# A hybrid mLSTM and GLA block: output gate units in another place, sigmoid and silu from tanh

## The chip, the cores and the metric

The kernel runs on one core of a Trainium2 chip. Its time is the device time of one execution in microseconds (us). Before the change the median of three runs is 948.4 us (947.27 to 948.83).

## The reference

A block of width 1024 on 512 tokens with 16 learned meta tokens ahead of them, so 528 columns are computed. After an RMS norm, one large projection feeds two mixers of four heads each. The first mixer is an mLSTM, the second a gated linear attention (GLA). Learned gates merge the two, an output projection and a SwiGLU channel mixer follow. What the change touches:

```python
mqk = jax.nn.silu(causal_depthwise_conv(jnp.concatenate([mq, mk], axis=-1), conv_w[l], conv_b[l]))
...
hm = mlstm_chunkwise(...)
hm = head_rmsnorm(from_chunks(hm), m_head_g[l]) * jax.nn.sigmoid(mo.astype(f32)).reshape(bsz, tp, M_HEADS, M_DV)
...
merged = (jax.nn.sigmoid(gate_m) * (y_m @ w_branch_m[l].astype(dt))
          + jax.nn.sigmoid(gate_g) * (y_g @ w_branch_g[l].astype(dt)))
```

`mq` and `mk` are the queries and keys of the first mixer, one tile of 128 channels per head; `mv` its values and `mo` its output gates, two tiles per head. Everything is fp32.

## The kernel before

The activations stand channel by channel: x transposed lies in eight tiles of 128 partitions by 528 columns. The weights come from HBM as 192 units of 128 x 1024, one for each 128 output channels, and the time goes into multiplying these units with the activations. An fp32 product is made of three matmuls (L302 to L304). For that every operand is split into a high part, rounded to fp32r, and the low rest. Of a weight unit, ACT makes the high part (`whi`, L188) and DVE the low part (`wlo`, L193), a few units ahead of PE. Some later products are done in pairs, with fewer matmuls on combinations of two units (L344 to L346). There ACT copies (`sink_of`, L404 to L409) empty a PSUM bank before PE can go on in it. There are 8 banks.

`job_list` (L52) writes down the order of the units: `gates`, then for each head of the first mixer `mq`, `mk`, two `mv`, two `mo`; then pairs for the merge gates (`gm`), the second mixer, its merge gates (`gg`), and so on. PE works through the units in this order.

All work that is not a unit's own matmuls is written as Python generators. `unit` (L308) advances them eight times while it issues its own 48 matmuls: `tick` (L153) gives a step to each generator in `side`, and to the first one in `mixers`. So the position of an instruction in its engine's order depends on the units that stand before it. Each engine executes its own order strictly one after the other: an instruction that waits holds up all that stand behind it on this engine.

The generators that matter here. `conv` (L705): the depthwise convolution of one query or key tile; the PSUM result goes to SBUF (L593, two halves on DVE), the first step runs on ACT, three more on DVE (L716). `conv_act` (L720): silu on ACT (L725) once query and key are there, then the high part on ACT (L730) and the low part on DVE (L732). `gates_of` (L610) scales an `mo` tile on DVE (L615) and applies its function on ACT. `normed_x` puts x's norm to use; its steps are L508 and L517 on DVE and L511 and a further one on ACT. `mlstm` (L867) is one head's mixer; it begins with an ACT cast of a constant selector, `sel` (L872), and six ticks later PE multiplies by it (L875, L876). `head_out` (L785) ends a head: head norm with Ln and Exp, times the gate. `branch` (L1081) multiplies a merge gate and a branch product.

ACT can apply one function only while a set of tables that holds it is loaded. `act` (L126) loads the set with Exp and Ln (an instruction at L130) where it is needed. The compiler puts in the loads for silu and sigmoid, which show up at L132, the line of the activation itself.

Of the kernel before, what the change touches and what calls it, by code (L numbers as in the profile page):

```python
# [8 lines left out]
F32 = mybir.dt.float32  # L9
# [6 lines left out]
P = 128  # L16
# [6 lines left out]
H = 4  # L23
# [22 lines left out]
NSTD = 6  # L46
HA = NT - 256
LOGEXP = "natural_log_exp_and_others"
TABLE = {AF.Exp: LOGEXP, AF.Ln: LOGEXP, AF.Silu: "silu", AF.Sigmoid: "sigmoid"}


def job_list():  # L52

    one = lambda *a: [(x,) for x in a]
    o = one(("gates", 0))
    for h in range(H):
        o += one(("mq", h), ("mk", h), ("mv", 2 * h), ("mv", 2 * h + 1), ("mo", 2 * h), ("mo", 2 * h + 1))
    two = lambda n, i: [((n, 2 * i), (n, 2 * i + 1))]
    g = lambda h: [(("gq", h), ("gk", h))] + two("gv", h) + two("gr", h)
    bm = lambda i: one(("bm", 2 * i), ("bm", 2 * i + 1))  # L60
    o += two("gm", 0) + two("gm", 1) + g(0) + two("gm", 2) + two("gm", 3)
    for i in range(4):
        o += bm(i)
    q, v, r = ([g(h)[i] for h in range(H)] for i in range(3))
    o += [q[1], v[1], q[2], r[1], v[2], q[3], v[3], r[2], r[3]]
    for i in range(4):
        o += two("gg", i)
    for i in range(8):
        o += one(("bg", i))
    for i in range(8):  # L70
        o += one(("out", i))
    for m in range(FT):
        o += one(("fg", m), ("fu", m)) if m < NSTD else [(("fg", m), ("fu", m))]
    for i in range(22):
        o += one(("down", i))
    return o
# [24 lines left out]
def hybrid_block(ctx: ExitStack, tc: tile.TileContext, xT, wst, par, con, out):  # L101
# [23 lines left out]

    def act(o, i, func, **kw):  # L126
        want = TABLE.get(func)
        if want is not None and want != table[0]:
            if want == LOGEXP:
                S.preload_act_table_set(want)  # L130
            table[0] = want
        S.activation(o, i, func, **kw)  # L132

    class Box:
# [251 lines left out]
    def sink_of(boxes, a_all, b_all, func=None):  # L386

        def sink(bz, bx, by):
            every = a_all or b_all
            n = lambda full: NT if full else NS  # L390
            a, b = tt(n=n(a_all)), tt(n=n(b_all))
            sa, sb = tt(), tt()
            h2 = slice(NM, HA) if every else slice(0, 256)
            h1 = lambda full: slice(0, HA) if full else h2
            m = lambda full: HA if full else 256

            def fin():
                if func is not None:
                    act(a, a, func)
                    act(b, b, func)  # L400
                boxes[0].v, boxes[1].v = a, b

            return dict(
                s1=lambda: S.copy(sa[:, :m(a_all)], bx[:, h1(a_all)]),  # L404
                s2=lambda: S.copy(sb[:, :m(b_all)], bx[:, h1(b_all)]),
                s5=lambda: S.copy(sa[:, HA:], bx[:, h2]),
                s7=lambda: S.copy(sb[:, HA:], bz[:, h2]),
                c11=lambda: V.tensor_tensor(a[:, :m(a_all)], by[:, h1(a_all)], sa[:, :m(a_all)], ALU.add),
                c12=lambda: S.copy(a[:, m(a_all):], bx[:, h2]),  # L409
                c21=lambda: V.scalar_tensor_tensor(b[:, :m(b_all)], bz[:, h1(b_all)], -1.0, sb[:, :m(b_all)],  # L410
                                                   ALU.mult, ALU.subtract),
                c22=lambda: V.scalar_tensor_tensor(b[:, m(b_all):], sa[:, HA:], -1.0, sb[:, HA:],
                                                   ALU.mult, ALU.subtract), fin=fin)
        return sink
# [195 lines left out]
    def gates_of(boxes, pss, func):  # L610
        ts = []
        for i, scale in pss:
            t = tt(n=NS)
            if scale is not None:
                V.tensor_tensor(t, i, scale[:, NM:], ALU.mult)  # L615
                i = t
                yield 1
            ts.append((t, i))
        for b, (t, i) in zip(boxes, ts):
            act(t, i, func)  # L620
            b.v = t


# [96 lines left out]
    def conv_act(q, k, src):  # L720
        while src[0].v is None or src[1].v is None:
            yield 1
        yield 2
        for b, a in ((q, src[0].v), (k, src[1].v)):
            act(a, a, AF.Silu)  # L725
        yield 1
        for b, a in ((q, src[0].v), (k, src[1].v)):
            n = a.shape[1]
            hi, lo = tt(F32R, n), tt(F32R, n)
            S.copy(hi, a)  # L730
            yield 2
            V.tensor_tensor(lo, a, hi.bitcast(F32), ALU.subtract)  # L732
            b.v = hi, lo
        src[0].v = src[1].v = None

# [49 lines left out]
    def head_out(num, d2, gcol, gates, hd, dst):  # L785
        s0, s1 = tt(n=NS), tt(n=NS)
        act(s0, num[0], AF.Square)
        act(s1, num[1], AF.Square)
        while gates[0].v is None or gates[1].v is None:
            yield 1  # L790
        yield 1
        ts = []
        for vt in range(2):
            f = 2 * hd + vt
            t = gates[vt].v
            V.scalar_tensor_tensor(t, num[vt], pr[:, gcol + f:gcol + f + 1], t, ALU.mult, ALU.mult)
            gates[vt].v = None
            ts.append(t)
            yield 1
        V.tensor_tensor(s0, s0, s1, ALU.add)  # L800
        yield 1
        sh, sl = tt(F32R, NS), tt(F32R, NS)
        S.copy(sh, s0)
        yield 2
        V.tensor_tensor(sl, s0, sh.bitcast(F32), ALU.subtract)
        yield 6
        ss = bank()
        T.matmul(ss, onesr, sh, start=True, stop=False)
        T.matmul(ss, onesr, sl, start=False, stop=True)
        yield 2  # L810
        x, y0, t = tt(n=NS), s0, s1
        if d2 is not None:
            V.scalar_tensor_tensor(x, d2, 256.0 * EPS, ss, ALU.mult, ALU.add)
        else:
            V.tensor_scalar(x, ss, 256.0 * EPS * QS2, None, op0=ALU.add)
        yield 1
        act(y0, x, AF.Ln, scale=1.0 / 256.0)
        yield 1
        act(y0, y0, AF.Exp, scale=-0.5)
        yield 1  # L820
        act(t, y0, AF.Square)
        yield 1
        V.scalar_tensor_tensor(t, t, -0.5 / 256.0, x, ALU.mult, ALU.mult)
        V.scalar_tensor_tensor(y0, t, 1.5, y0, ALU.add, ALU.mult)
        yield 1
        for vt in range(2):
            y = ts[vt]
            if dst is yg and hd > 0:
                y = hpool[0].tile([P, NS], F32, tag="h", name=nm("h"))
            V.tensor_tensor(y, ts[vt], y0, ALU.mult)  # L830
            dst[2 * hd + vt] = y
            yield 1

# [117 lines left out]


    atts = []
    nega = cpool.tile([P, H], F32, name="nega")
    S.mul(nega, pr[:, C_A2B:C_A2B + H], -1.0)

# [123 lines left out]

    def branch(box, ps, sg, add=None, parts=None):  # L1081
        t = sg.v
        V.tensor_tensor(t, ps, t, ALU.mult)
        if add is not None:
            V.tensor_tensor(t, t, add.v, ALU.add)
            add.v = None
        box.v = t
        sg.v = None
        yield 1
        if parts is not None:  # L1090
            hi, lo = tt(F32R, NS), tt(F32R, NS)
            S.copy(hi, t)
            yield 1
            V.tensor_tensor(lo, t, hi.bitcast(F32), ALU.subtract)
            parts[0].append(hi)
            parts[1].append(lo)
            box.v = None
# [24 lines left out]
    def hold(what, i, boxes, func):  # L1122

        held[what] = held.get(what, []) + [unit_real((what, i))]
        if i % 2:
            run(gates_of(boxes, held.pop(what), func))
# [39 lines left out]
    for job in JOBS[2:]:  # L1166
# [3 lines left out]
        if len(job) == 2:  # L1170
# [7 lines left out]
            if what == "gq":  # L1178
                pair(job, X.w, ALL, sink_of((b.q, b.k), False, True))
            elif what == "gv":  # L1180
                pair(job, X.w, ALL, sink_of(b.vf, True, True))
            elif what == "gr":
                pair(job, X.w, REAL, sink_of(b.gates, False, False, AF.Silu))
            else:
                if what == "gg" and i == 6:
                    run(some_parts(yg, 2))
                elif what == "gm" and i == 4:
                    run(some_parts(ym, 4))
                pair(job, X.w, REAL, sink_of({"gm": gm, "gg": gg}[what][i:i + 2], False, False, AF.Sigmoid))
        elif what == "mq":  # L1190
            b = head("m", i)
            b.src = [box(), box()]
# [17 lines left out]
                fetch_mix()  # L1210
                fetch_mix()
        elif what == "mo":
            hold(what, i, head("m", i // 2).gates, AF.Sigmoid)
        elif what == "bm":
            while not hpool:
                tick()
# [392 lines left out]
```

## Time and profile before

| | |
|---|---|
| median of 3 runs | 948.4 us (947.27 to 948.83) |
| profiled execution, its own time | 948.52 us |
| span in the profile | 946.7 us |
| PE busy | 917.5 us |
| DVE busy | 636.2 us |
| ACT busy | 546.2 us |
| POOL busy | 86.8 us |
| mean granted clock of TensorE | 0.992 |

PE is TensorE's matmuls, DVE VectorE, ACT ScalarE, POOL GpSimd. The span reaches from the first to the last instruction. A busy share is an average over all stages; whether an engine holds up the time is read from what waits for it. The granted clock is what the chip let TensorE run at, as a share of its full speed of 2.4 GHz; 0.50 is its lower level, 1.2 GHz.

### The profile page before, as it was taken

To read this page: it belongs to the slowest core of one execution; us is meant where nothing else is said; L and a number is where in the kernel's file an instruction comes from. 1 tells how busy PE (TensorE), PEld (TensorE's weight loads), DVE (VectorE), ACT (ScalarE), POOL (GpSimd) and SP (SyncE) were. 2 spreads that over 40 slices of the span, in tenths; PEclk is the share of its full clock that TensorE was granted. 3 is DMA by queue.
4 is the path that set the end of the run, shared out by engine and by line. 5 is a ranking of instruction groups with operands and counts; after the bars stand their busy time and mean duration, and the time that the engine had idled before them with its cause. 6 is when DMAs were issued, how large, how long until landed. Compare 5 with 4: busy or idle time off the path is not lost.

```text
span 946.7 us, 15478 instructions
## 1 busy us (share of the span) xinstructions
PE 917.5 (97%) x6083; PEld 842.3 (89%) x6083; DVE 636.2 (67%) x940; ACT 546.2 (58%) x954; POOL 86.8 (9%) x102
## 2 busy tenths in 40 slices
PE   6999999989999999999999999999999999999995
PEld 6988899878998899999998888888999999888885
DVE  6797776767875577777777556785767767842323
ACT  7557788779684256766874334443555555732321
POOL 0000022001100011110100000212121110000000
PEclk9999999989999999999999999999999999999998
DMA  7245375345562466655643343335788885322302
GB/s 262 101 139 155 119 162 123 75 112 134 127 163 90 111 148 155 163 120 141 134 134 107 116 133 116 107 102 132 185 186 179 189 191 148 115 94 85 111 1 89
DMA packets 48712, 124.45 MB, mean 131 GB/s; under 512 B 5376, under 2 KB 11520, under 8 KB 48640
## 3 DMA queue, kind: packets, MB, share of 16 engines
q1 hardware_dynamic: 35008, 101.32, 34.5%
q0 software_dynamic: 12544, 21.11, 14.5%
q8 instruction: 47, 0.77, 0.3%
q10 hardware_dynamic: 1088, 1.05, 0.3%
q14 instruction: 25, 0.20, 0.1%
HBM read 118.08 MB, written 5.37 MB: 130 GB/s over the span
## 4 chain that ended last, share of the span: by engine, by line
PE 78%; ACT 9%; DVE 8%; issue 3%; DMA 1%; DVEq 0%; SPq 0%; ACTq 0%
PE b L303 13%; PE b L302 13%; PE b L304 13%; PE b L344 12%; PE b L345 11%; PE b L346 11%; ACT t L132 4%; ACT whi L188 2%; DVE wlo L193 1%; ACT L130 1%; PE b L1056 1%; DVE t L716 1%; PE b L1058 1%; PE b L1035 1%; ACT L132 1%
## 5 line engine op out<-in xcount | busy, mean ns | idle before, releaser
L303 PE MATMUL b<-t,whi 128*128 128x512 f32 (+2 forms) x822 | 289.9, 353 | 1.0 <-DVE t L471 0.7
L302 PE MATMUL b<-t,whi 128*128 128x512 f32 (+2 forms) x774 | 274.0, 354 | 6.7 <-ACT t L132 6.6
L304 PE MATMUL b<-t,wlo 128*128 128x512 f32 (+2 forms) x774 | 270.8, 350 | 0.0
L344 PE MATMUL b<-t,whi 128*128 128x256 f32 (+1 forms) x864 | 250.0, 289 | 7.7 <-ACT t L404 6.1
L346 PE MATMUL b<-t,wlo 128*128 128x256 f32 (+1 forms) x864 | 245.1, 284 | 0.0
L345 PE MATMUL b<-t,whi 128*128 128x256 f32 (+1 forms) x864 | 245.0, 284 | 0.0
L193 DVE TENSOR_TENSOR wlo<-raw,whi 128x1024 fp32r<-128x1024 f32 x155 | 193.1, 1249 | 50.8 <-ACT whi L188 50.5
L188 ACT CAST whi<-raw 128x1024 fp32r<-128x1024 f32 x155 | 161.7, 1047 | 64.5 <-PE b L345 27.4
L303 PEld LDWEIGHTS b<-t,whi 128*128 128x128 f32 x822 | 155.8, 190 | 23.3 <-DVE t L843 1.1
L344 PEld LDWEIGHTS b<-t,whi 128*128 128x128 f32 x864 | 164.3, 190 | 9.9 <-ACT t L404 7.2
L302 PEld LDWEIGHTS b<-t,whi 128*128 128x128 f32 x774 | 147.0, 190 | 26.5 <-ACT t L132 6.6
L345 PEld LDWEIGHTS b<-t,whi 128*128 128x128 f32 x864 | 164.3, 190 | 0.5
L304 PEld LDWEIGHTS b<-t,wlo 128*128 128x128 f32 x774 | 146.8, 190 | 19.9 <-DVE wlo L193 0.3
L346 PEld LDWEIGHTS b<-t,wlo 128*128 128x128 f32 x864 | 164.0, 190 | 0.0
L132 ACT ACTIVATE t<-t 128x512 f32<-128x512 f32 (+6 forms) x124 | 70.4, 588 | 29.8 <-DVE t L1289 9.3
L183 POOL DMA_DIRECT2D raw<-wst x36 | 31.2, 867 | 364.4 <-DMA wf<-wst 104.9
L188 ACT CAST whi<-wf 128x1024 fp32r<-128x1024 f32 x36 | 37.8, 1051 | 22.5 <-PE b L345 13.5
L132 ACT ACTIVATE t<-f 128x256 f32<-128x256 f32 (+1 forms) x24 | 11.6, 482 | 61.6 <-DVE f L1456 61.6
L212 POOL DMA_DIRECT2D wf<-wst x36 | 32.5, 912 | 155.3 <-DMA wf<-wst 85.7
L193 DVE TENSOR_TENSOR wlo<-wf,whi 128x1024 fp32r<-128x1024 f32 x36 | 43.9, 1218 | 0.0
L1456 DVE TENSOR_TENSOR f<-f,b 128x512 f32<-128x512 f32 (+1 forms) x9 | 5.7, 629 | 53.3 <-PE b L304 53.3
L344 PE MATMUL b<-t,wgh 128*128 128x256 f32 (+1 forms) x144 | 41.0, 285 | 0.0
(219 smaller groups left out, 1216.6 us busy)
## 6 DMA issues: line engine op xcount, KB each, us to landing
raw<-wst SPq DMA_DIRECT2D x155, 512.0 KB, 3.6
wf<-wst SPq DMA_DIRECT2D x36, 256.0 KB, 3.2
wf<-wst POOLq DMA_DIRECT2D x36, 256.0 KB, 5.4
raw<-wst POOLq DMA_DIRECT2D x36, 256.0 KB, 4.7
t<-xT SPq DMA_DIRECT2D x8, 264.0 KB, 5.6
pos<-t SPq DMA_DIRECT2D x8, 264.0 KB, 2.3
t<-xT SPq DMA_DIRECT2D x8, 256.0 KB, 3.8
t<-neg POOLq DMA_DIRECT2D x6, 272.0 KB, 6.3
```

What stands on the lines that cost most here:

```text
L130: S.preload_act_table_set(want)
L132: S.activation(o, i, func, **kw)
L183: G.dma_start(lr(r, 0), lr(wst[v - 1], 0), accum_op=ALU.add)
L188: S.copy(t, src)
L193: V.tensor_tensor(t, src, hi.bitcast(F32), ALU.subtract)
L212: G.dma_start(lr(st.f, 1), lr(wst[u + 1], 1), accum_op=ALU.add)
L302: T.matmul(o, w_h, ah[:, c0:c1], start=first, stop=False)
L303: T.matmul(o, w_h, al[:, c0:c1], start=False, stop=False)
L304: T.matmul(o, w_l, ah[:, c0:c1], start=False, stop=last)
L344: T.matmul(o, h, xh_[k][:, c0:c1], start=start and k == 0, stop=False, skip_group_check=not start)
L345: T.matmul(o, h, xl_[k][:, c0:c1], start=False, stop=False, skip_group_check=not start)
L346: T.matmul(o, l, xh_[k][:, c0:c1], start=False, stop=k == 3, skip_group_check=not start)
```

## The change

It does four things.

The order of the units: the `mo` units of head h no longer follow its `mv` units. They follow `mq` and `mk` of head h+1, and those of the last head stand at the end of the first mixer.

Sigmoid is computed as (tanh(x/2) + 1)/2 for `mo`, `gm` and `gg`. The + 1 is taken in where the gate is multiplied anyway (head_out, branch), by a DVE instruction with a scalar (scalar_tensor_tensor) in place of a plain one; the 1/2 goes into a halved gain (`halfg`, one new small ACT instruction) or into the split that follows.

Silu of the first mixer's queries and keys becomes a tanh into a new tile and a new DVE instruction (t + 1) * a, eight of them in all; the 1/2 goes into the high and low part. The second mixer's `gr` gates and the channel mixer keep silu.

`act` now knows that Exp is in two sets, with Ln or with Tanh, and loads a set only if the present one lacks the function. The number of table loads in the program goes from 35 to 27.

```diff
@@ -46,15 +46,19 @@
 NSTD = 6
 HA = NT - 256
 LOGEXP = "natural_log_exp_and_others"
-TABLE = {AF.Exp: LOGEXP, AF.Ln: LOGEXP, AF.Silu: "silu", AF.Sigmoid: "sigmoid"}
+TANHEXP = "exp_and_others"
+
+TABLE = {AF.Exp: (LOGEXP, TANHEXP), AF.Ln: (LOGEXP,), AF.Tanh: (TANHEXP,), AF.Silu: ("silu",)}
 
 
 
     one = lambda *a: [(x,) for x in a]
     o = one(("gates", 0))
+    mo = lambda h: one(("mo", 2 * h), ("mo", 2 * h + 1))
     for h in range(H):
-        o += one(("mq", h), ("mk", h), ("mv", 2 * h), ("mv", 2 * h + 1), ("mo", 2 * h), ("mo", 2 * h + 1))
+        o += one(("mq", h), ("mk", h)) + (mo(h - 1) if h else []) + one(("mv", 2 * h), ("mv", 2 * h + 1))
+    o += mo(H - 1)
     two = lambda n, i: [((n, 2 * i), (n, 2 * i + 1))]
     g = lambda h: [(("gq", h), ("gk", h))] + two("gv", h) + two("gr", h)
     bm = lambda i: one(("bm", 2 * i), ("bm", 2 * i + 1))
@@ -125,10 +129,10 @@
 
     def act(o, i, func, **kw):
         want = TABLE.get(func)
-        if want is not None and want != table[0]:
-            if want == LOGEXP:
-                S.preload_act_table_set(want)
-            table[0] = want
+        if want is not None and table[0] not in want:
+            table[0] = want[0]
+            if func != AF.Silu:
+                S.preload_act_table_set(want[0])
         S.activation(o, i, func, **kw)
 
     class Box:
@@ -396,8 +400,8 @@
 
             def fin():
                 if func is not None:
-                    act(a, a, func)
-                    act(b, b, func)
+                    for x in (a, b):
+                        act(x, x, func, scale=0.5 if func == AF.Tanh else 1.0)
                 boxes[0].v, boxes[1].v = a, b
 
             return dict(
@@ -617,7 +621,7 @@
                 yield 1
             ts.append((t, i))
         for b, (t, i) in zip(boxes, ts):
-            act(t, i, func)
+            act(t, i, func, scale=0.5)
             b.v = t
 
 
@@ -722,14 +726,17 @@
             yield 1
         yield 2
         for b, a in ((q, src[0].v), (k, src[1].v)):
-            act(a, a, AF.Silu)
+            t = tt(n=a.shape[1])
+            act(t, a, AF.Tanh, scale=0.5)
+            V.scalar_tensor_tensor(a, t, 1.0, a, ALU.add, ALU.mult)
+            del t
         yield 1
         for b, a in ((q, src[0].v), (k, src[1].v)):
             n = a.shape[1]
             hi, lo = tt(F32R, n), tt(F32R, n)
-            S.copy(hi, a)
+            act(hi, a, AF.Copy, scale=0.5)
             yield 2
-            V.tensor_tensor(lo, a, hi.bitcast(F32), ALU.subtract)
+            V.scalar_tensor_tensor(lo, a, 0.5, hi.bitcast(F32), ALU.mult, ALU.subtract)
             b.v = hi, lo
         src[0].v = src[1].v = None
 
@@ -793,7 +800,10 @@
         for vt in range(2):
             f = 2 * hd + vt
             t = gates[vt].v
-            V.scalar_tensor_tensor(t, num[vt], pr[:, gcol + f:gcol + f + 1], t, ALU.mult, ALU.mult)
+            if dst is ym:
+                V.scalar_tensor_tensor(t, t, 1.0, num[vt], ALU.add, ALU.mult)
+            else:
+                V.scalar_tensor_tensor(t, num[vt], pr[:, gcol + f:gcol + f + 1], t, ALU.mult, ALU.mult)
             gates[vt].v = None
             ts.append(t)
             yield 1
@@ -827,7 +837,10 @@
             y = ts[vt]
             if dst is yg and hd > 0:
                 y = hpool[0].tile([P, NS], F32, tag="h", name=nm("h"))
-            V.tensor_tensor(y, ts[vt], y0, ALU.mult)
+            if dst is ym:
+                V.scalar_tensor_tensor(y, ts[vt], halfg[:, 2 * hd + vt:2 * hd + vt + 1], y0, ALU.mult, ALU.mult)
+            else:
+                V.tensor_tensor(y, ts[vt], y0, ALU.mult)
             dst[2 * hd + vt] = y
             yield 1
 
@@ -951,6 +964,8 @@
 
 
     atts = []
+    halfg = cpool.tile([P, 8], F32, name="halfg")
+    S.mul(halfg, pr[:, C_MG:C_MG + 8], 0.5)
     nega = cpool.tile([P, H], F32, name="nega")
     S.mul(nega, pr[:, C_A2B:C_A2B + H], -1.0)
 
@@ -1080,7 +1095,7 @@
 
     def branch(box, ps, sg, add=None, parts=None):
         t = sg.v
-        V.tensor_tensor(t, ps, t, ALU.mult)
+        V.scalar_tensor_tensor(t, t, 1.0, ps, ALU.add, ALU.mult)
         if add is not None:
             V.tensor_tensor(t, t, add.v, ALU.add)
             add.v = None
@@ -1089,9 +1104,9 @@
         yield 1
         if parts is not None:
             hi, lo = tt(F32R, NS), tt(F32R, NS)
-            S.copy(hi, t)
-            yield 1
-            V.tensor_tensor(lo, t, hi.bitcast(F32), ALU.subtract)
+            act(hi, t, AF.Copy, scale=0.5)
+            yield 1
+            V.scalar_tensor_tensor(lo, t, 0.5, hi.bitcast(F32), ALU.mult, ALU.subtract)
             parts[0].append(hi)
             parts[1].append(lo)
             box.v = None
@@ -1186,7 +1201,7 @@
                     run(some_parts(yg, 2))
                 elif what == "gm" and i == 4:
                     run(some_parts(ym, 4))
-                pair(job, X.w, REAL, sink_of({"gm": gm, "gg": gg}[what][i:i + 2], False, False, AF.Sigmoid))
+                pair(job, X.w, REAL, sink_of({"gm": gm, "gg": gg}[what][i:i + 2], False, False, AF.Tanh))
         elif what == "mq":
             b = head("m", i)
             b.src = [box(), box()]
@@ -1210,7 +1225,7 @@
                 fetch_mix()
                 fetch_mix()
         elif what == "mo":
-            hold(what, i, head("m", i // 2).gates, AF.Sigmoid)
+            hold(what, i, head("m", i // 2).gates, AF.Tanh)
         elif what == "bm":
             while not hpool:
                 tick()
```

**ACT, at the start of head 0's mixer.** Line numbers of the changed kernel are 4 higher at the start of the file and 13 at this mixer. First the order before, from the cast of a part of normed x down to `sel` (`t_779` is the convolution of head 1's query, `t_681` and `t_689` are head 0's output gates):

```order
L511 CAST t_699<-t_679 128x528
L132 ACTIVATE t_702<-t_679 128x272
L132 ACT_TABLE_LOAD
L132 ACTIVATE t_681<-t_681 128x512
L132 ACTIVATE t_689<-t_689 128x512
L132 ACTIVATE t_779<-t_769,pr 128x512
L188 CAST whi_788<-raw_618 128x1024
L511 CAST t_791<-t_767 128x528
L132 ACTIVATE t_794<-t_767 128x272
L872 CAST sel_799<-cn 128x256
```

The same place after (`t_797` and `t_801` receive the tanh of head 1's query `t_678` and key `t_750`, `t_808` and `t_823` their high parts):

```order
L192 CAST whi_756<-raw_567 128x1024
L515 CAST t_758<-t_741 128x528
L136 ACTIVATE t_761<-t_741 128x272
L135 ACT_TABLE_LOAD
L136 ACTIVATE t_797<-t_678 128x512
L136 ACTIVATE t_801<-t_750 128x528
L136 ACTIVATE t_808<-t_678 128x512
L136 ACTIVATE t_823<-t_750 128x528
L192 CAST whi_829<-raw_651 128x1024
L515 CAST t_832<-t_817 128x528
L136 ACTIVATE t_835<-t_817 128x272
L885 CAST sel_839<-cn 128x256
```

The gates of head 0 are gone from ahead of `sel`, and both tanh and both high parts of head 1 now stand there, as do the first steps of its two convolutions (`t_678` and `t_750` receive them; those rows stand further up).

**DVE, at the same place.** Before; the L593 rows bring head 1's query out of PSUM, L615 scales head 0's gates:

```order
L508 SCALAR_TENSOR_TENSOR t_679<-t_77,pr,t_317 128x528
L615 TENSOR_TENSOR t_681<-b_558,t_317 128x512
L615 TENSOR_TENSOR t_689<-b_617,t_317 128x512
L193 TENSOR_TENSOR wlo_726<-raw_559,whi_697 128x1024
L517 TENSOR_TENSOR t_700<-t_679,t_699 128x528
L508 SCALAR_TENSOR_TENSOR t_767<-t_79,pr,t_317 128x528
L707 MEMSET t_769 128x3
L593 TENSOR_TENSOR t_769<-b_669,t_317 128x264
L593 TENSOR_TENSOR t_769<-b_670,t_317 128x264
L716 SCALAR_TENSOR_TENSOR t_779<-t_769,pr,t_779 128x512
L693 COPY acol<-b_714 128x480
L716 SCALAR_TENSOR_TENSOR t_779<-t_769,pr,t_779 128x512 x2
```

After, from the evacuation of head 1's key (`t_743`) on; the two L731 are the new instruction:

```order
L597 TENSOR_TENSOR t_743<-b_649,t_319 128x264
L597 TENSOR_TENSOR t_743<-b_650,t_319 128x264
L720 SCALAR_TENSOR_TENSOR t_750<-t_743,pr,t_750 128x528 x3
L197 TENSOR_TENSOR wlo_779<-raw_567,whi_756 128x1024
L521 TENSOR_TENSOR t_759<-t_741,t_758 128x528
L731 SCALAR_TENSOR_TENSOR t_678<-t_797,t_678 128x512
L731 SCALAR_TENSOR_TENSOR t_750<-t_801,t_750 128x528
L512 SCALAR_TENSOR_TENSOR t_817<-t_79,pr,t_319 128x528
L739 SCALAR_TENSOR_TENSOR t_809<-t_678,t_808 128x512
L697 COPY acol<-b_769 128x480
L739 SCALAR_TENSOR_TENSOR t_824<-t_750,t_823 128x528
L197 TENSOR_TENSOR wlo_848<-raw_651,whi_829 128x1024
```

All of head 1's convolution and the new products now come ahead of the L512 for `t_817`, whose cast stands on ACT ahead of `sel`; the gates of head 0 follow later.

**ACT, at the end of the first mixer.** Before, around the last head's start (`t_2302` and `t_2303` are its output gates, `t_2293` and `t_2294` the copies that free banks of a pair):

```order
L769 CAST t_1738<-b_2279 128x256
L132 ACT_TABLE_LOAD
L132 ACTIVATE t_2302<-b_2122 128x512
L132 ACTIVATE t_2303<-b_2206 128x512
L879 COPY t_2329<-b_2319 128x512
L188 CAST whi_2338<-raw_2123 128x1024
L130 ACT_TABLE_LOAD
L132 ACTIVATE t_2331<-b_2320,cb 128x512
L404 COPY t_2293<-b_2289 128x256
L407 COPY t_2294<-b_2288 128x256
```

After, the same stretch:

```order
L776 CAST t_1809<-b_2296 128x256
L136 ACTIVATE t_2319<-b_2139 128x512
L136 ACTIVATE t_2320<-b_2223 128x512
L892 COPY t_2346<-b_2336 128x512
L192 CAST whi_2355<-raw_2140 128x1024
L136 ACTIVATE t_2348<-b_2337,cb 128x512
L408 COPY t_2310<-b_2306 128x256
L411 COPY t_2311<-b_2305 128x256
```

Both loads are gone. A little further down, after:

```order
L136 ACTIVATE t_2416<-t_2347,acol 128x128
L192 CAST whi_2422<-raw_2067 128x1024
L135 ACT_TABLE_LOAD
L136 ACTIVATE t_2262<-t_2410 128x512
L921 CAST wh_2365<-t_2371 128x512
L136 ACTIVATE t_2416<-t_2346,acol 128x128 x2
```

The load stands ahead of the Ln of a head's norm (`t_2262<-t_2410`), which had none ahead of it at this place before.

## Rows read from the trace of the kernel before

**Rows 1.** The page: the span, busy time, share and number of instructions of PE, PEld, DVE, ACT and POOL, and the chain that ended last by engine.

```profile
span 946.7 us, 15478 instructions
...
PE 917.5 (97%) x6083; PEld 842.3 (89%) x6083; DVE 636.2 (67%) x940; ACT 546.2 (58%) x954; POOL 86.8 (9%) x102
...
PE 78%; ACT 9%; DVE 8%; issue 3%; DMA 1%; DVEq 0%; SPq 0%; ACTq 0%
```

**Rows 2.** The waits of PE: the line that waits, what it waited for; us in total, how many times, the longest in us.

```profile
PE b L302 <- ACT t L132: 6.6, 1, 6.6
PE b L344 <- ACT t L404: 6.1, 4, 3.6
PE b L875 <- ACT sel L872: 1.9, 1, 1.9
PE b L939 <- DVE t L757: 1.6, 1, 1.6
PE b L344 <- ACT t L405: 1.1, 1, 1.1
...
PE b L748 <- ACT t L591: 0.5, 1, 0.5
```

**Rows 3.** Two windows of 20 us, the second the one with most DVE work between 80 and 240 us: busy us (and instructions) of PE, PEld, DVE, ACT, POOL, the granted clock, the DMA engines' share, GB/s.

```profile
60.00:80.00 20.00, 18.00 (x139) 17.24 (x138) 18.48 (x30) 14.01 (x25) 0.00 (x0) 1.00 0.54 178
120.00:140.00 20.00, 20.00 (x132) 18.20 (x130) 15.36 (x29) 16.25 (x34) 4.86 (x4) 1.00 0.73 162
```

**Rows 4.** The timeline of DVE: start in us, us, the instruction; in brackets the idle time before it and what ended it.

```profile
43.36 0.70 DVE L649 TENSOR_TENSOR t<-t,t 32x528 f32<-32x528 f32 x1 [3.13 <-ACT t L132]
...
55.56 1.21 DVE L193 TENSOR_TENSOR wlo<-raw,whi 128x1024 fp32r<-128x1024 f32 x1
...
62.21 1.27 DVE L615 TENSOR_TENSOR t<-b,t 128x512 f32<-128x512 f32 x2
...
65.16 0.75 DVE L508 SCALAR_TENSOR_TENSOR t<-t,pr,t 128x528 f32<-128x528 f32 x1
65.85 0.41 DVE L593 TENSOR_TENSOR t<-b,t 128x264 f32<-128x264 f32 x1
...
67.48 0.75 DVE L716 SCALAR_TENSOR_TENSOR t<-t,pr,t 128x512 f32<-128x512 f32 x1 [0.89 <-ACT t L132]
```

**Rows 5.** The timeline of ACT ahead of head 0's `sel`, and PE at L875, columns as above.

```profile
66.63 0.82 ACT L132 ACTIVATE t<-t,pr 128x512 f32<-128x512 f32 x1 [0.89 <-DVE t L593]
67.36 1.03 ACT L188 CAST whi<-raw 128x1024 fp32r<-128x1024 f32 x1
68.29 0.63 ACT L511 CAST t<-t 128x528 fp32r<-128x528 f32 x1
...
69.16 0.39 ACT L872 CAST sel<-cn 128x256 fp32r<-128x256 f32 x1
...
69.60 0.50 PE L875 MATMUL b<-t,sel 128*128 128x512 f32 x1 [1.87 <-ACT sel L872]
```

**Rows 6.** Windows of 2 us around the waits at 68 and 196, columns as in the third group.

```profile
68.00:70.00 2.00, 0.40 (x2) 0.36 (x3) 1.96 (x4) 2.00 (x6) 0.00 (x0) 1.00 0.00 0
198.00:200.00 2.00, 0.29 (x1) 0.29 (x2) 1.25 (x2) 1.99 (x5) 0.00 (x0) 0.58 0.79 123
200.00:202.00 2.00, 2.00 (x10) 2.00 (x10) 0.67 (x1) 1.79 (x6) 0.00 (x0) 0.50 1.09 232
202.00:204.00 2.00, 2.00 (x9) 1.81 (x9) 0.49 (x2) 0.67 (x2) 0.00 (x0) 0.50 0.46 180
204.00:206.00 2.00, 2.00 (x13) 2.00 (x13) 1.02 (x3) 0.38 (x1) 0.00 (x0) 0.71 0.00 0
```

**Rows 7.** ACT's groups by line and shape: the table loads; count, busy us and mean ns of one, then idle time before them.

```profile
L130 ACT ACT_TABLE_LOAD x17 | 21.8, 1283 | 0.3
L132 ACT ACT_TABLE_LOAD x17 | 21.8, 1283 | 0.3
```

**Rows 8.** The timeline of ACT ahead of the copy of L404 for which PE waits until 199.7.

```profile
193.59 1.28 ACT L132 ACT_TABLE_LOAD   x1
194.89 1.09 ACT L132 ACTIVATE t<-b 128x512 f32<-128x512 f32 x2
...
196.32 1.07 ACT L188 CAST whi<-raw 128x1024 fp32r<-128x1024 f32 x1
197.41 1.28 ACT L130 ACT_TABLE_LOAD   x1
198.71 0.69 ACT L132 ACTIVATE t<-b,cb 128x512 f32<-128x512 f32 x1
199.29 0.36 ACT L404 COPY t<-b 128x256 f32<-128x256 f32 x1
```

**Rows 9.** Timelines further on: ACT at the Ln, a load, DVE behind the Ln, and PE at 243.84.

```profile
205.62 1.05 ACT L188 CAST whi<-raw 128x1024 fp32r<-128x1024 f32 x1 [2.27 <-PE b L345]
206.57 0.63 ACT L132 ACTIVATE t<-t 128x512 f32<-128x512 f32 x1
...
235.15 1.28 ACT L130 ACT_TABLE_LOAD   x1
...
210.54 0.69 DVE L823 SCALAR_TENSOR_TENSOR t<-t,t 128x512 f32<-128x512 f32 x1 [1.07 <-ACT t L132]
...
243.84 0.40 PE L344 MATMUL b<-t,whi 128*128 128x272 f32 x1 [0.88 <-ACT t L404]
```

## The prediction

> **What bounds the kernel now.** I read the page first: in a span of 946.7 us PE is busy for 917.5, DVE for 67% and ACT for 58%, and the chain that ended last is 78% PE [rows 1]. So the time is the matmul work plus what PE stands still or runs at half clock, and the matmul work is the same after the change: an edit counts only where it lengthens or shortens a wait of PE. Next I read the waits of PE [rows 2]. The 6.6 us at the start come before any changed line. What is left between 60 and 250 us, where all edited work that could matter lies, is small: 1.9 us on the `sel` cast of L872, 1.6 on a DVE product of L757, 6.1 on four copies of L404, 1.1 on one of L405, 0.5 on L591. Then I read the places where these waits stand, engine by engine in order of time. The profiled execution took 948.52 us, 0.12 above the median of the runs shown (948.4), so 1.8 of it lies outside the span; I sum against 948.5 and take 0.1 off at the end.
>
> **Table loads.** A load takes 1.283 us, 17 by L130 and 17 by L132 [rows 7]. Tanh and Exp share a set, so 35 loads become 27, all eight saved ahead of 250 us; that is 10.3 us of ACT, but ACT is idle 42% of the span, and only loads that stand in a chain that PE waits for count. There are two such chains.
>
> At 195.7 PE waits 3.6 us for the copy of L404 that frees a bank. Ahead of it on ACT stand a load (193.59), two sigmoids, `whi`, another load (197.41) and the Exp of L132, and each instruction starts as the last one ends [rows 8]. Both loads go: 2.57 us less, and the wait becomes 3.6 − 2.57 = 1.0. This wait also cost clock: the granted clock is 0.50 from 200 to 204 and 0.71 from 204 to 206 [rows 6], so that after PE resumed at 199.7 it lost 0.15 + 2.0 + 0.58 = 2.7 us. After the waits of 1.9 and 1.6 us the clock stayed at 1.00 (the first is in [rows 6]), so I count the 2.7 as won: 5.3 in all here.
>
> A load comes in new ahead of the Ln at 206.57, because Ln isn't in the set of Tanh [rows 9]. DVE waits for that activation's successors (1.07 us at 210.54), its later work releases the casts ahead of the L404 copy on which PE waits 1.1 us at 214 [rows 9]. ACT is shown waiting for DVE there, so I let all 1.28 through: this wait becomes 2.4. Bounds: nothing, if the 2.27 us in which ACT waited for PE at 205.62 absorb it, and 1.28. The wait of 1.1 on L405 stays, since a load stands ahead of it as before. The one of 0.88 at 243.84 loses a load of 1.28 at 235.15 [rows 9]; between nothing and 0.88 I take 0.3, since ACT also waits for DVE in between. The last head's Ln gets a new load too, and between nothing and 1.28 I put 0.4 on it, nearer to nothing because no wait of PE stands there. Sum from 190 us on: before 3.6 + 2.7 + 1.1 + 1.1 + 0.9 = 9.4, after 1.0 + 2.4 + 1.1 + 0.3 + 0.4 = 5.2, a gain of **4.2 us** (2 to 6).
>
> On a single point the Trainium skill speaks against this. "ScalarE: Activation LUTs", section "What ACT_TABLE_LOAD costs", says that every switch of set also costs a drain of about 1.38 us, some 2.66 in all. The rows here don't show it: the load at 197.41 starts as `whi` ends and the next activation starts 0.02 after the load's end. By the page the two loads would give 5.3 and the new one would cost 2.7, by the rows 2.57 and 1.28. The sum goes by [rows 8].
>
> **The moved units.** This is the dearer part. Before, head 0's `sel` cast stands on ACT right behind the convolution of the next head's query, a `whi` and two small steps; PE comes to L875 at 67.73 and waits 1.87 us for it [rows 5]. After, the query and key units of head 1 come two units earlier, so their whole convolution and activation stand ahead of `sel` on ACT: two tanh, two copies for the high part, and on DVE four evacuations (L593), six convolution steps (L716), and two of the new products. PE's place in its own order is unchanged, so it still arrives at 67.7.
>
> DVE has no room for this: it is busy 18.48 of the 20 us from 60 to 80 [rows 3], and with no gap named from 55.56 to the L593 at 65.85 [rows 4]. From the `wlo` at 55.56 to the end of the L508 at 65.16 it took 10.29 us. After, that stretch loses the two scalings of head 0's gates by L615 (1.20, start to start) and gains four L593 (4 × 0.345 = 1.38), six L716 (6 × 0.72 = 4.35) and two new products (1.45, at the size of L716): 16.3. Two waits for the convolution's first step on ACT (0.89 as at 67.48) add some 1.5, and head 0's two new products start all of it some 0.7 late (half of 1.45, the other half falls into the 3.13 us for which DVE waited at 43.36). The last new product comes before one L508 (0.7) and so ends at 55.56 + 0.7 + 16.3 + 1.5 − 0.7 = 73.4. On ACT follow the copy of the key's high part (0.6), `whi` (0.95), the cast and negation of a mask row (0.87), and `sel` (0.39) [rows 5]: 76.2. PE waits 76.2 − 67.7 = 8.5 us instead of 1.87: **+6.6**. A wait of 3.6 was enough for half clock, so this one costs clock as well; I take the same 2.7: **+2.7**.
>
> Bounds. Below: if DVE's order leaves slack that I don't see, the wait stays 1.9 and nothing is added. Above: 8.5 and a clock loss with all later waits kept, +9.3. Against it stands that all other engines catch up in those 8 us: the waits of 1.6 on L757 and 0.5 on L591 [rows 2], both ahead of 190 us, go: **−2.1** (0 to −2.1). Heads 2 and 3 have their 1.45 us more of DVE in stretches where it is busy 15.4 us of 20 at most [rows 3]; that idle time hides them, and I cost them at nothing. The same for the halved gain (one ACT instruction on 8 columns), for the products of head_out and branch, whose count is unchanged, and for everything behind 250 us, where no load changes and the matmuls hide a product of 0.7 us; if that cover were gone, the first mixer's eight products would cost 6 us.
>
> Sum: 948.5 − 4.2 + 6.6 + 2.7 − 2.1 = 951.5, less 0.1 for the median: **951.4**.
>
> **The rivals.**
> Faster: the early wait doesn't grow. For it: `sel` itself reads only constants, so ACT's order alone holds it up, and ACT is idle for 0.89 us before 66.63 [rows 5]. Against: that idle time ended on DVE, whose load grows. Then 948.5 − 4.2 − 2.1 to 948.5 − 4.2: 942.2 to 944.3. Chance 0.16.
> No difference: the wait of 8.5 comes, but without the loss of clock or with a shorter one, since ACT and DVE run ahead meanwhile: 948.5 + 6.6 − 2.1 − 4.2 = 948.8; a clock loss of up to 1.5 stays within 950.3. Chance 0.24.
> Slower than forecast: the Ln's new load makes the wait at 214 long enough (2.4; 1.9 didn't, 3.6 did) for a second loss of clock. The price is 2.7 again, and it decides from a wait of about 2.7 on, half-way between the two: 954.1. Chance 0.13.
> The page's drain: in my rows the four waits from 190 us would be 0, 3.7 (with 2.7 of clock), 1.1 and under 1, 7.8 or so, a gain of 1.6 in place of 4.2: 954.0. The rows give no gap; chance 0.03.
> The forecast: 0.44. A measurement of this kernel tells 0.2%, 1.9 us, from no change: 946.5 to 950.3. The forecast's own spread (949 to 953.5) puts a fifth of it within that. Faster 0.17 (the first rival and a little of the spread), same 0.32, slower 0.51. The range for 8 in 10 goes from 944.5, which leaves out most of the faster rival, to 955.0.
>
> **What would show it.** Right: one wait of PE on the `sel` cast of 6 to 9 us near 68, followed by a granted clock of 0.5; DVE busy without a gap from 56 to 73; the wait at 196 at 1 us or less with the clock at 1.00; the one near 214 above 2. Wrong: a wait on `sel` under 3 us, which makes it faster, or a clock that stays at 1.00 behind a long wait, which makes it the same. If PE's busy time at full clock changed, the ground of the whole sum would be wrong.

## The result and the profile after

The changed kernel takes 950.58 us, the median of nine runs (949.75 to 952.09), beside 947.93 for the kernel before on the same chip (nine runs, 946.86 to 948.83). The ratio is 1.0029, 95% interval 1.0019 to 1.0040: slower by 2.7 us, where 951.4 us and 3.0 more were forecast. The profiled execution took 952.09 us, the slowest of the nine, so differences between the two traces come out somewhat larger than between the medians.

The page of the changed kernel, lines that answer to [rows 1]:

```profile
span 950.2 us, 15475 instructions
...
PE 919.2 (97%) x6083; PEld 843.5 (89%) x6083; DVE 641.5 (68%) x949; ACT 536.7 (56%) x945; POOL 86.8 (9%) x102
...
PE 85%; ACT 6%; DVE 6%; issue 1%; DMA 1%; SPq 0%; DVEq 0%; ACTq 0%
```

The span grew by 3.5 us. ACT is busy 9.5 us less, DVE 5.3 us more, and PE is busy 1.7 us more with the same 6083 matmuls, part of which run at a lower clock. The waits of PE, as in [rows 2]:

```profile
PE b L888 <- ACT sel L885: 8.3, 1, 8.3
PE b L306 <- ACT t L136: 7.0, 2, 6.8
PE b L348 <- ACT t L408: 2.8, 2, 2.3
PE b L307 <- DVE t L475: 1.4, 2, 0.7
```

The wait on `sel` (now L885) grew from 1.9 to 8.3 us. The bank copies (L404, now L408) fell from 6.1 to 2.8. The wait on L757's product and the one on L405 are gone. About 1.0 us of the growth (6.6 to 6.8, and a second wait of 0.7 on L475) stands at the start, ahead of every place that the change touches.

Windows of 2 us around the two long waits, columns as in [rows 3]:

```profile
76.00:78.00 2.00, 0.71 (x2) 0.62 (x3) 2.00 (x4) 1.99 (x6) 0.00 (x0) 0.50 0.42 159
78.00:80.00 2.00, 2.00 (x10) 1.91 (x9) 2.00 (x5) 1.54 (x3) 0.00 (x0) 0.50 0.85 218
80.00:82.00 2.00, 2.00 (x14) 1.96 (x13) 2.00 (x5) 2.00 (x4) 0.00 (x0) 0.79 0.64 246
216.00:218.00 2.00, 0.52 (x2) 0.52 (x3) 2.00 (x3) 1.70 (x4) 0.56 (x1) 0.84 0.41 33
218.00:220.00 2.00, 2.00 (x12) 2.00 (x11) 2.00 (x5) 1.03 (x4) 0.00 (x0) 0.50 0.92 214
222.00:224.00 2.00, 2.00 (x11) 2.00 (x11) 0.91 (x5) 2.00 (x5) 0.87 (x1) 0.50 0.73 205
224.00:226.00 2.00, 2.00 (x18) 2.00 (x17) 1.70 (x5) 1.32 (x3) 0.00 (x0) 0.95 0.85 154
```

Twice the granted clock is at its lower level of 1.2 GHz while PE is back at work. Behind `sel` that costs 0.36 + 1.0 + 0.42 = 1.8 us (busy time times what is missing of the clock), and behind the wait that ended at 217.48 another 0.26 + 3.0 + 0.1 = 3.4, with the window from 220 on like its two neighbours. Before, there was one such stretch, from 199.7 to 206 [rows 6], which cost 2.7.

Next the ACT timeline of the changed kernel ahead of `sel`, the place of [rows 5], with PE at L888:

```profile
68.20 0.83 ACT L136 ACTIVATE t<-t,pr 128x528 f32<-128x528 f32 x1 [3.71 <-DVE t L597]
...
70.84 1.28 ACT L135 ACT_TABLE_LOAD   x1
72.13 1.17 ACT L136 ACTIVATE t<-t 128x512 f32<-128x512 f32 x2
73.82 1.32 ACT L136 ACTIVATE t<-t 128x512 fp32r<-128x512 f32 x2 [0.52 <-DVE t L731]
75.05 1.03 ACT L192 CAST whi<-raw 128x1024 fp32r<-128x1024 f32 x1
...
76.85 0.39 ACT L885 CAST sel<-cn 128x256 fp32r<-128x256 f32 x1
...
77.29 0.80 PE L888 MATMUL b<-t,sel 128*128 128x512 f32 x1 [8.33 <-ACT sel L885]
```

DVE at the same time, the place of [rows 4]:

```profile
69.06 2.38 DVE L720 SCALAR_TENSOR_TENSOR t<-t,pr,t 128x528 f32<-128x528 f32 x3 [0.90 <-ACT t L136]
...
73.10 1.30 DVE L731 SCALAR_TENSOR_TENSOR t<-t,t 128x512 f32<-128x512 f32 x2
...
75.61 0.65 DVE L697 COPY acol<-b 128x480 f32<-128x480 f32 x1
```

ACT waits 0.52 us for the first new product (L731), then the high parts, a `whi`, a cast and a negation run one behind the other down to `sel`. DVE has no idle time from 69.06 on; the 0.90 us ahead of that is its wait for the convolution's first step on ACT. Both engines are about 8 us late against PE here.

ACT at the end of the first mixer, the places of [rows 8] and [rows 9]:

```profile
202.09 0.69 ACT L136 ACTIVATE t<-b,cb 128x512 f32<-128x512 f32 x1
202.67 0.37 ACT L408 COPY t<-b 128x256 f32<-128x256 f32 x1
...
207.67 1.28 ACT L135 ACT_TABLE_LOAD   x1
208.96 0.63 ACT L136 ACTIVATE t<-t 128x512 f32<-128x512 f32 x1
...
217.48 0.58 PE L348 MATMUL b<-t,whi 128*128 128x256 f32 x1 [2.32 <-ACT t L408]
```

Both loads ahead of the copy at 202.67 are gone, and so is all but 0.14 us of the wait. The load that came in at 207.67 stands ahead of the Ln, and the wait at 217.48 answers to the 1.09 us at 215.10 before.

By the traces: the wait on `sel` +6.5, half clock behind it +1.8, smaller waits up to 190 us −1.3 (2.2 before, 0.9 after), everything from 190 to 260 us −3.5 (6.7 of waits and 2.7 of clock before, 2.5 and 3.4 after), the start +1.0. That makes +4.5 against 3.5 measured in the spans; 1.0 us is not accounted for.

### The profile page after: what moved, and what is told of

Read it like the earlier page. It is cut to its first block, busy times and chain, and to the rows that moved or that the text cites. A ratio compares the mean times of both kernels' runs of the same rounds, so it can differ in the third digit from the quotient of the medians.

```text
span 950.2 us, 15475 instructions
## 1 busy us (share of the span) xinstructions
PE 919.2 (97%) x6083; PEld 843.5 (89%) x6083; DVE 641.5 (68%) x949; ACT 536.7 (56%) x945; POOL 86.8 (9%) x102
## 4 chain that ended last, share of the span: by engine, by line
PE 85%; ACT 6%; DVE 6%; issue 1%; DMA 1%; SPq 0%; DVEq 0%; ACTq 0%
PE b L306 14%; PE b L307 14%; PE b L308 14%; PE b L348 12%; PE b L349 12%; PE b L350 12%; ACT t L136 3%; ACT whi L192 1%; ACT L135 1%; PE b L1071 1%; DVE t L720 1%; PE b L1073 1%; DVE wlo L197 1%; PE b L1050 1%; DMA t<-xT 1%
## 5 line engine op out<-in xcount | busy, mean ns | idle before, releaser
L136 ACT ACTIVATE t<-t 128x512 f32<-128x512 f32 (+6 forms) x139 | 79.8, 593 | 57.9 <-DVE t L1100 27.8
```

## The experiments

Two theories were held against each other: the order of the units makes the early wait and the table loads the late gain, or the eight new products on DVE make the loss. Each time is set against the kernel before, which was run in turn with it.

**The order alone.** The kernel before, with the new `job_list` and nothing else.

```diff
-        o += one(("mq", h), ("mk", h), ("mv", 2 * h), ("mv", 2 * h + 1), ("mo", 2 * h), ("mo", 2 * h + 1))
+        o += one(("mq", h), ("mk", h)) + (mo(h - 1) if h else []) + one(("mv", 2 * h), ("mv", 2 * h + 1))
+    o += mo(H - 1)
```

> The kernel before with the new order of the units alone (sigmoid and silu as before, 35 table loads). Theory (the order brings head 1's convolution ahead of head 0's sel cast, the new products only add to it): PE waits 6.1 us on sel, 2.2 less than in the changed kernel, and loses 1.8 us of clock behind it; the wait near 196 with its clock loss stays, as both table loads ahead of it stay. Time 950 to 953, 951.9 likeliest. Rival (the new DVE products make the early wait): the wait on sel stays under 3 us, time 946 to 948.5.

Measured: 952.69 us, ratio 1.0059 (1.0046 to 1.0072). Two waits of PE, the first from the list of waits, the second from the timeline:

```profile
PE b L877 <- ACT sel L874: 7.1, 1, 7.1
...
204.25 0.39 PE L346 MATMUL b<-t,whi 128*128 128x256 f32 x1 [2.76 <-ACT t L406]
```

The wait on `sel` is 7.1 us, so the order makes 5.2 of the 6.5 us by which it grew, and the tanh with its products 1.2. The theory holds, its term of 2.2 for the products was too large. The late wait stays, with both loads ahead of it, but is 2.76 and not 3.59, and the half clock behind it costs 1.6 us and not 2.7.

**Tanh alone.** The changed kernel with the old `job_list` (the diff above the other way round).

> The changed kernel with the old order of the units: tanh and the saved table loads, but output gates directly behind their head's values. Theory: the wait on sel is 1.9 to 3.2 us, the wait near 196 is under 1 us with no loss of clock, a wait of about 2.3 us with a loss of clock comes near 215 from the Ln's table load. Time 943.5 to 946.5, 945 likeliest. Rival (the new products on DVE cost what the loads give): 947 to 950.

Measured: 942.62 us, ratio 0.9951 (0.9939 to 0.9964), faster than forecast and than both kernels. Its waits of PE:

```profile
PE b L346 <- ACT t L406: 2.8, 2, 2.3
PE b L886 <- ACT sel L883: 2.2, 1, 2.2
PE b L346 <- ACT t L407: 1.3, 1, 1.3
```

The three waits are as the theory has them: 2.2 on `sel`, 2.3 at the Ln's load, none near 196. Half clock came behind the wait on `sel` (1.7 us), but not behind that of 2.3 at 209.87:

```profile
208.00:210.00 2.00, 0.13 (x1) 0.13 (x2) 2.00 (x4) 2.00 (x6) 0.81 (x1) 1.00 0.23 37
210.00:212.00 2.00, 2.00 (x18) 2.00 (x19) 2.00 (x5) 0.73 (x4) 0.00 (x0) 1.00 0.89 215
```

The clock is 1.00 in all the windows behind it in which PE works. The changed kernel has the same wait with 3.4 us of half clock. The theory had half clock here as well, and its likeliest time was 2.4 us too high. The new products cost no wait of their own.

**The sel cast early.** The changed kernel, one cast moved ahead of the loop that waits for query and key.

```diff
+        sel = mpool.tile([P, 2, P], F32R, tag="sel", name=nm("sel"))
+        S.copy(sel, cn[:, NS + h:NS + 8:H].unsqueeze(2).to_broadcast([P, 2, P]))
         while not gts.ready or q.v is None or k.v is None:
             yield 1
         (qh, ql), (kh, kl) = q.v, k.v
-        sel = mpool.tile([P, 2, P], F32R, tag="sel", name=nm("sel"))
-        S.copy(sel, cn[:, NS + h:NS + 8:H].unsqueeze(2).to_broadcast([P, 2, P]))
```

> The changed kernel with one line moved: the sel cast, which reads only constants, is issued when a head's mixer is first advanced, not after its query and key are there. Theory (PE waits at 68 for nothing but ACT's order): the wait of 8.3 us and 1.8 us of clock go, some of the small waits on DVE and on banks come back since PE is then ahead of DVE; time 941 to 946, 943.5 likeliest. Rival (DVE's backlog itself bounds that stretch): a wait of 5 us or more on a wlo or on an evacuation takes its place within 20 us; time 948 to 950.6.

Measured: 949.65 us, ratio 1.0028 (1.0016 to 1.0039). The rival was right in kind. PE and DVE at the place:

```profile
68.88 0.39 PE L888 MATMUL b<-t,sel 128*128 128x512 f32 x1
76.38 0.80 PE L889 MATMUL b<-t,sel 128*128 128x512 f32 x1 [7.11 <-DVE acol L697]
...
75.67 0.65 DVE L697 COPY acol<-b 128x480 f32<-128x480 f32 x1
```

L888 no longer waits, but the very next matmul, L889, does, for 7.1 us: it needs a PSUM bank, and the one that would be free holds the columns that DVE copies to `acol` at 75.67, behind head 1's convolution and products. `sel` was the name of the wait; behind it stood the backlog of both engines. Half clock costs 2.9 us behind this wait and 1.7 near 218, against 1.8 and 3.4 in the changed kernel.

**The norm's last steps later.** The changed kernel with two more ticks between the Square and the DVE instruction that reads it.

```diff
         act(t, y0, AF.Square)
-        yield 1
+        yield 3 if dst is ym else 1
```

> The changed kernel with the last steps of the head norm two ticks later (the DVE instruction that waits for the activations behind the Ln then stands behind the evacuation for the next wh cast). Theory (the Ln's table load reaches PE through DVE's order): the wait of 2.3 us near 215 falls to about 0.9 and the half clock behind it, worth 3.2 us, does not come; time 945 to 947.5, 945.9 likeliest; the wait on sel is unchanged at 8.3. Rival (the load reaches PE through ACT's own order): the wait near 215 stays above 2 and the time within 1 us of the changed kernel.

Measured: 952.65 us, ratio 1.0060 (1.0047 to 1.0074). The first half of the theory holds, the gain does not:

```profile
215.79 0.39 PE L348 MATMUL b<-t,whi 128*128 128x256 f32 x1 [0.74 <-ACT t L408]
...
223.64 0.58 PE L348 MATMUL b<-t,whi 128*128 128x256 f32 x1 [2.98 <-ACT t L409]
...
219.03 0.42 ACT L921 CAST wh<-t 128x272 fp32r<-128x272 f32 x1 [3.03 <-DVE t L917]
...
220.68 1.28 ACT L135 ACT_TABLE_LOAD   x1
...
223.22 0.36 ACT L409 COPY t<-b 128x256 f32<-128x256 f32 x1
```

The wait near 215 fell to 0.74 as forecast. But PE then reached the next copy (L409) early, and waited 2.98 for it: ACT had waited 3.03 us for a DVE product behind the postponed steps, and the load of the tanh table stands ahead of that copy as well. The wait moved by 8 us and grew, and half clock came behind it there, for 1.5 us.

**Without the Ln.** The changed kernel with an Identity where the Ln of the first mixer's norm was, so that no table has to change there; this leaves out the logarithm.

```diff
-        act(y0, x, AF.Ln, scale=1.0 / 256.0)
+        act(y0, x, AF.Identity if dst is ym else AF.Ln, scale=1.0 / 256.0)
```

> The changed kernel with the Ln of the first mixer's head norm replaced by an Identity activation of the same size, so that its table load and the one back to Tanh are not needed; this leaves the logarithm out of the head norm. Theory (the Ln's load makes the wait near 215): that wait falls from 2.3 to about 1 us and its half clock does not come; time 944.5 to 947.5, 946 likeliest; the wait on sel stays at 8.3. Rival (the wait near 215 comes from the chain of the wh casts, not from the load): it stays above 1.8 us and the time within 1.5 us of the changed kernel.

Measured: 945.9 us, ratio 0.9983 (0.9974 to 0.9991). PE at the place:

```profile
213.73 0.38 PE L348 MATMUL b<-t,whi 128*128 128x256 f32 x1 [1.06 <-ACT t L408]
```

The wait at 213.73 is 1.06, against 2.32 in the changed kernel: 1.26 less, one load of 1.283 us. No half clock follows. In ratios the kernel gains 0.46%, 4.4 us, about the 1.3 of the wait and the 3.4 of clock together. So without the new load the second stretch of half clock does not come. Tanh alone, which has the load and no half clock there, shows that the load by itself is not enough for it.

**Normed x later.** As the run with `sel` early, and the side work on x's norm four units later.

```diff
-            if i == 1:
-                run(normed_x())
-            elif i == 4:
+            if i == 4:
...
             elif i == 2:
+                run(normed_x())
```

> As the run with sel issued early, and in addition the side work that forms normed x (one DVE product, an ACT cast and negation, a DVE low part for each of eight tiles) starts four units later, with head 1's first value unit and not with head 0's second. Theory (what PE waits for at 68 is the end of a backlog on DVE and ACT, whichever semaphore is named): about five of these tiles leave the stretch from 55 to 76, 6.5 us of DVE, and the wait of 7.1 us on the acol copy falls to under 1.5 us without a loss of clock; time 940 to 945, 942 likeliest. Rival (head 1's convolution alone is enough for the backlog): the wait stays at 4 us or more; time 947 to 950.

Measured: 953.85 us, ratio 1.0070 (1.0056 to 1.0084). The wait on the `acol` copy fell from 7.1 to 3.3 us, between the two forecasts: the backlog is shared between normed x and the convolution. Half clock still followed (2.8 us). PE's waits on what the move put late, and on the copies behind it:

```profile
PE b L348 <- ACT t L408: 3.5, 2, 3.0
...
PE b L348 <- ACT t L409: 2.6, 2, 2.1
PE b L349 <- ACT t L584: 1.2, 1, 1.2
PE b L350 <- DVE wlo L197: 1.1, 1, 1.1
PE b L348 <- ACT t L584: 1.1, 1, 1.1
```

The casts of the mixed inputs (L584) and the copies behind them now come late, and there are new waits of 1.1, 1.2, 3.0, 2.1 and 1.1 us between 198 and 258, with 3.0 us of half clock among them. More than was gained came back.

**The same with the old order.** Old `job_list`, tanh, `sel` early, normed x four units later.

> The old order of the units with tanh, and in addition sel issued early and normed x four units later. Theory: the wait of 2.2 us near 68 and the 1.7 us of half clock behind it go; time 938 to 941, 939 likeliest. Rival (the moved work makes a wait of its own between 80 and 120 us): a new wait of 2 us or more there; time 941.5 to 945.

Measured: 951.25 us, ratio 1.0037 (1.0024 to 1.0050). Near 68 no wait and no half clock is left, as the theory has it. But waits of 1.1, 1.2, 3.1, 2.1 and 1.1 us stand between 193 and 254, with 2.8 us of half clock, where the rival had 80 to 120. Neither had looked that far: what normed x feeds, the mixed inputs, is cast some 125 us later, and these casts now stand among the bank copies on ACT.

**The load one step earlier.** Old order, tanh, and the set with Ln loaded one step ahead.

```diff
         if d2 is not None:
+            if table[0] != LOGEXP:
+                S.preload_act_table_set(LOGEXP)
+                table[0] = LOGEXP
             V.scalar_tensor_tensor(x, d2, 256.0 * EPS, ss, ALU.mult, ALU.add)
```

> The old order of the units with tanh, and the table load for the head norm's Ln issued one step earlier, ahead of an activation and a whi on ACT for which ACT waits for PE. Theory: the idle time of 0.85 us in front of that whi takes part of the load, the wait of 2.3 us near 210 falls to about 1.5; time 941 to 942.5, 941.8 likeliest. Rival (ACT has no idle time there once PE is not slowed): the wait stays at 2.3 and the time at 942.6.

Measured: 941.97 us, ratio 0.9938 (0.9925 to 0.9950). The wait is 1.55 us, as forecast. In time it can't be told from tanh alone, whose interval overlaps.

**And sel early.** To that the moved `sel` cast.

> The old order of the units with tanh, the Ln's table load one step earlier, and the sel cast issued early; normed x stays where it was. Theory: as in the run with sel issued early alone, PE then waits for the bank that the acol copy on DVE frees; that copy ends about 0.7 us before sel did, so the wait near 69 falls from 2.2 to about 1.5 us and the 1.7 us of half clock behind it may go; time 939.5 to 941.5, 940.5 likeliest. Rival (sel alone makes the wait): under 0.5 us there, 938 to 939.5.

Measured: 940.65 us, ratio 0.9927 (0.9915 to 0.9940). The wait near 69 is 1.26 us, on the `acol` copy, and its half clock is gone. But half clock now comes behind the wait on the bank copy, which ends at 207.41 and is 1.55 us long, as in the run before:

```profile
209.00:210.00 1.00, 1.00 (x6) 1.00 (x6) 1.00 (x2) 1.00 (x4) 0.00 (x0) 0.50 0.92 275
```

It costs 1.7 us, as much as went at 72. In time the intervals of this run and the one before overlap.

**And normed x one unit later.** One line more:

```diff
         nh, nl = [], []
+        yield 8
```

> The same, and normed x started one unit later instead of four. Theory (the backlog near 68 shrinks by one tile of normed x, 1.3 us of DVE, and the mixing casts of L582 come only 5 us later): the wait near 69 is under 0.7 us without half clock, no wait on L582 near 195; time 938 to 940, 939 likeliest. Rival (any shift of normed x brings the waits near 195 back): two waits of 1 us or more on those casts, time 942 to 946.

Measured: 939.34 us, ratio 0.9913 (0.9900 to 0.9927): 8 us below the kernel before, the fastest of all. It was run in turn with the one before, and their times do not overlap (938.86 to 939.96 against 940.53 to 940.88). PE's waits:

```profile
PE b L346 <- ACT t L406: 2.1, 2, 1.6
PE b L912 <- DVE t L763: 1.1, 1, 1.1
...
PE b L891 <- DVE acol L696: 0.5, 1, 0.5
```

The wait on the `acol` copy is 0.52 and no wait on the mixing casts appears. With the old order one unit of shift is enough for the backlog, and four had cost more than they gave.

## Why the prediction was right

The forecast was +3.0 us and the measured difference is +2.7. Its reason was the right one: the early wait on `sel` outweighs the table loads. That the sum came so near is in part luck, since terms were off by 0.7 to 0.9 us in both directions. The steps, one by one. (Two slips in the working change nothing: the wait near 196 began at 196.1 and not at 195.7, and six steps of 0.72 are 4.3 and not 4.35.)

That PE's waits set the time. Right: both kernels and the last run issue the same 6083 matmuls, and where waits and half clock went, time went.

The wait on `sel`, 8.5: it is 8.33. The last new product ended at 74.4 and not at 73.4, and PE came at 68.96 and not at 67.73, since this execution started later; the two shifts cancel. The rival without growth is excluded, and the order alone gives 7.1. What the prediction didn't see is what else stood behind this wait: it had DVE's backlog reach PE through ACT's order alone, and the run with `sel` early shows that DVE's `acol` copy would have held PE by itself for 7.1 us.

Half clock behind it, 2.7: it is 1.8. The smaller waits that go, 2.1: 1.3.

The wait near 196, 3.6 to 1.0 without its half clock: it fell to 0.14. Two loads explain 2.57 of the 3.45. The rest, 0.9, goes with either edit: the order alone, with both loads still there, takes 0.83 off the wait, and tanh alone, in the old order, leaves 0.12 of it. In both, ACT stands idle for PE at a cast some instructions ahead of that copy (0.53 and 0.26 us), where it ran without a gap before, so it comes to this place less late.

The wait near 215, 2.4: 2.32, and the run without the Ln shows that the load alone makes the difference. The forecast and its rival with a drain are told apart by the same run: removing the load took 1.26 from the wait, and in the row at 207.67 the next activation starts 1.29 us after the load did. The Trainium skill, "ScalarE: Activation LUTs", section "What ACT_TABLE_LOAD costs", would have 2.66 us for a switch of set; the traces here don't agree with that.

The step that failed: that a wait of 2.4 us leaves the clock at 1.00, taken from a line between 1.9 and 3.6 us. Half clock came behind a wait of 2.32 and cost 3.4 us; the slower rival, with a chance of 0.13, had it at 2.7. And the waits of 1.1 on L405, 0.3 at 243 and 0.4 at the last head's Ln that were kept in the sum did not appear. For the one on L405 the runs suggest a link: a PE at half clock comes to the next copy later and finds it ready. Where half clock followed the wait on the bank copy (the changed kernel, `sel` early, the last two runs), PE did not wait for that next copy. Where it stayed away (tanh alone, and the load one step earlier), PE waited 1.28 us for it. So the sum from 190 us on, a gain of 4.2, came out as 3.5 by wrong terms of opposite sign, and that is luck.

That the new products cost nothing outside the early stretch. Right: in tanh alone no wait on them is named.

What stays open: why the two edits together lose 2.7 us, where their single effects (+5.6 and −4.6 by the ratios) add up to 1.0. In the traces the half clock does not add up. From 190 to 230 us it costs 2.7 before, 1.6 with the order alone, nothing with tanh alone and 3.4 with both. Near 70 it goes the other way: each edit alone costs 1.7 there, and both together 1.8. No run shows why it comes behind the wait near 215 with both edits and not with tanh alone.

## What to carry to other kernels

When a wait is named after one small instruction, look at how far its engine and the next one are behind at that moment; moving the instruction alone passes the wait to the next resource that the same backlog delays, here a PSUM bank. When a unit of work is moved ahead, count all the side work that comes ahead with it on the engines that already run without a gap, and follow what the work that is pushed back feeds, even 125 us later. Take two edits apart before judging them: here one alone is worth −0.5% and the other +0.6%.

## What was not expected of the hardware

Whether a wait of PE costs clock was not decided by its length. A wait of 1.57 us on the bank copy was followed by half clock in the last run (1.7 us lost), one of 2.31 on the same copy in tanh alone was not, and one of 1.87 on `sel` before was not. The wait of 1.55 on the bank copy was followed by it in the run before the last (1.7 us lost), and not in the run that had the load one step earlier and `sel` in its old place. The windows of the last run:

```profile
206.00:208.00 2.00, 1.76 (x12) 1.77 (x13) 2.00 (x5) 0.73 (x3) 0.00 (x0) 0.84 0.70 88
208.00:210.00 2.00, 2.00 (x12) 2.00 (x11) 2.00 (x4) 1.98 (x6) 0.00 (x0) 0.50 0.62 182
210.00:212.00 2.00, 2.00 (x16) 2.00 (x16) 0.94 (x3) 1.99 (x5) 0.87 (x1) 0.81 0.37 59
```

The wait ended at 206.24, and a mean clock of 0.84 from 206 to 208 puts the fall at about 207.4 (0.32 of the two us missing, at half clock 0.64 us), with PE at work again. In the tanh-alone run the same happened behind the `sel` wait of 2.2 us: PE worked again from 70.72, and the clock was 0.52 from 72 to 74.

```profile
70.00:72.00 2.00, 1.28 (x8) 1.19 (x9) 1.97 (x3) 1.42 (x5) 0.00 (x0) 1.00 0.32 78
72.00:74.00 2.00, 2.00 (x12) 2.00 (x11) 2.00 (x4) 0.00 (x0) 0.00 (x0) 0.52 0.73 254
74.00:76.00 2.00, 2.00 (x10) 1.77 (x10) 1.43 (x6) 0.87 (x2) 0.00 (x0) 0.63 0.35 135
```

So half clock can begin when PE is busy again, and a short wait can cost more than its own length.
